# First-half projections in token order, the local recurrence stage ahead of the second half's projections, the triangular solve spread over later work, and a new order of products in two attentions

## The chip, the cores and the metric

The kernel runs on one core of one Trainium2 chip. The metric is device time in microseconds (us), from launch to end. Engines are named as the profile names them: PE (TensorE, matrix products) with PEld (its weight loads), DVE (VectorE), ACT (ScalarE), POOL (GpSimd), SP (SyncE, which here only issues DMAs). An instruction on one engine's list runs in the order in which it stands there; DMAs issued on one engine's queue are issued in order too, and an issue that must wait for its data holds back all that stand behind it.

## The reference

Two blocks, float32, 512 tokens of width 1024. The first has two layers (a neighbourhood attention A, a grouped attention B, each with a gated update behind it, "ple" in the kernel). The second is one hybrid layer: a sparse attention ("nsa") and an RWKV-7 recurrence, both fed by one projection of the same normalized activations. The change touches mainly the recurrence:

```python
prev = jnp.pad(p, ((0, 0), (1, 0), (0, 0)))[:, :-1]
p = p + shift_mu * (prev - p)                       # token shift
r, k, v, wd, ad = _split(p, (512, 512, 512, 64, 64))
w = (w0 + jnp.tanh(wd) @ w_up)                      # low-rank decay
decay = jnp.exp(-jnp.exp(-jax.nn.softplus(-w) - 0.5))
a = jax.nn.sigmoid(a0 + ad @ a_up)                  # low-rank rate
kk = heads(k * k_k); kk = kk / max(norm(kk), 1e-12)
k = k * (1.0 + (a - 1.0) * k_a)
# per token: sa = S @ -kk;  S = S*decay + sa (x) (kk*a) + v (x) k;  y = S @ r
```

## The kernel before, in words

Precision is kept by splitting each operand into a high part (`float32r`) and the rest, the low part, so that a product of activations and weights is three matmuls (high by high, high by low, low by high). A weight unit of 512 KB is loaded on SP's queue into `wraw`, ACT rounds it to `whi` (L147), and the engine in `self.lo` subtracts to get `wlo` (L148): DVE or POOL.

The program is written with tiles. A planner orders each engine's list once, before the run, from simulated costs: work emitted earlier has the higher priority, but work emitted later may be put ahead where an engine would otherwise be free in the plan. The order is then fixed.

The tokens of the first block stand in an order of their own (token 64*r + c at place 8*c + r). The recurrence needs them in natural order. `natural` (L322) rewrites the activations into it: 16 copies, eight on DVE and eight on ACT. The sequence of the stages that matter:

1. The end of the last ple (`middle_norm` gives the activations `act`, t being a block of 128 tokens).
2. `rwkv_proj_first` (L804): r, k and v of the first four heads (half 0, `hh` = 0) from the tokens in their own order, 2 x 48 matmuls of 256 columns for each of the three (`group_rows`, two token blocks at a time, `tp`). Each result is copied by ACT (L796), multiplied by `mu` on DVE (L797) and subtracted on POOL (L798), to stay in two tiles until eight DMAs (L812) write it to `d_raw`, with the order of tokens put right by the address pattern.
3. `rwkv_lowrank` (L747): 24 matmuls of 512 columns, the token shift, then eight low-rank products (L769), each with a tanh on ACT and a store to `d_low` on ACT's queue, through two buffers.
4. r of the second four heads (half 1), then in the next scope `rwkv_consts` (L724; it also writes zeros to `d_t` with eight DMAs on SP's queue, L736), k and v of half 1, `natural`.
5. `rwkv_local` (L827), eight times (`hh` = 0, 1; t = 0 to 3): it loads `low` from `d_low` (L837) and two shifted views of r, k, v from `d_raw` (L841), adds them (L844), normalizes, forms cumulative decays, and masks small products into `d_a` and others. It is a long chain that goes back and forth between DVE, ACT, POOL and PE. POOL makes the low parts of the weights here.
6. `rwkv_triangles` loads `d_a` (L951) and `rwkv_solve` (L957) inverts 128 triangles of 32 by 32 on DVE in 31 steps of two or four instructions (L967, L969), all emitted in one go; the result goes to `d_t` on ACT's queue.
7. `products()`: nsa's blocks, compression (L1186), keys, the gates of the recurrence, nsa's queries and scores. Between its pieces `tail` places the steps of the recurrence's `chain` (from `d_t`) by a list of numbers, the first behind piece 10.
8. `nsa_group` for two groups, then the output projection.

Attention B (`b_block`, L648) and nsa (`nsa_block`, L1337) transpose probabilities in pairs, split them (ACT the high part `ph`, then DVE the low part `pl`, L222), and multiply: block 0 high, block 0 low, block 1 high, block 1 low (L677, L1373).

## Time and profile before

| what | us |
|---|---|
| median of three runs | 1224.47 (1223.39 to 1226.15) |
| the profiled execution | 1225.36 |
| its span, first to last instruction | 1223.6 |
| busy in the span: PE, DVE, ACT, POOL | 1138.2, 851.1, 623.0, 395.8 |
| mean granted TensorE clock | 0.969 of full speed |

A busy PE is not PE at its peak: matmuls overlap, and the end of each is modelled, so that a PE waiting between two matmuls can still count as busy. How many matmuls start in a stretch tells more. A clock of 1.00 is 2.4 GHz, 0.5 is 1.2 GHz.

### The profile page before, as it was taken

To read this page: it belongs to the slowest core of one execution; us is meant where nothing else is said; L and a number is where in the kernel's file an instruction comes from. 1 tells how busy PE (TensorE), PEld (TensorE's weight loads), DVE (VectorE), ACT (ScalarE), POOL (GpSimd) and SP (SyncE) were. 2 spreads that over 40 slices of the span, in tenths; PEclk is the share of its full clock that TensorE was granted. 3 is DMA by queue.
4 is the path that set the end of the run, shared out by engine and by line. 5 is a ranking of instruction groups with operands and counts; after the bars stand their busy time and mean duration, and the time that the engine had idled before them with its cause. 6 is when DMAs were issued, how large, how long until landed. Compare 5 with 4: busy or idle time off the path is not lost.

```text
span 1223.6 us, 20514 instructions
## 1 busy us (share of the span) xinstructions
PE 1138.2 (93%) x7176; PEld 999.8 (82%) x7176; DVE 851.1 (70%) x2093; ACT 623.0 (51%) x1355; POOL 395.8 (32%) x549
## 2 busy tenths in 40 slices
PE   7999999998999989999999999799899799899896
PEld 5898989886889868877877898688789688798785
DVE  6566666657677877886676763489786925688865
ACT  5566565635443566566564642434444223267743
POOL 0021211110300364674311011164445523357731
PEclk9999999999999989999999999899799989899998
DMA  6333333213232310211132445774667553712511
GB/s 248 117 98 102 102 103 102 92 61 132 93 108 74 97 38 1 70 35 36 52 130 69 139 120 192 219 262 145 202 189 195 162 140 106 237 45 71 180 52 69
DMA packets 87040, 143.24 MB, mean 117 GB/s; under 512 B 21525, under 2 KB 52245, under 8 KB 86938
## 3 DMA queue, kind: packets, MB, share of 16 engines
q1 hardware_dynamic: 72344, 133.49, 34.3%
q10 hardware_dynamic: 14018, 6.36, 2.0%
q0 software_dynamic: 576, 2.10, 0.5%
q8 instruction: 56, 0.92, 0.3%
q14 instruction: 46, 0.38, 0.1%
HBM read 114.12 MB, written 27.79 MB: 116 GB/s over the span
## 4 chain that ended last, share of the span: by engine, by line
PE 61%; DVE 17%; DMA 7%; ACT 5%; issue 5%; POOL 3%; SPq 2%; ACTq 0%; POOLq 0%; DVEq 0%
PE mm L205 23%; PE mm L188 5%; PE mm L189 5%; PE mm L190 4%; PE sc L205 3%; PE mm L216 2%; DVE KT L967 2%; PE tr L492 1%; PE u L677 1%; PE tr L670 1%; DMA rkv<-d_raw 1%; PE ch L1003 1%; DVE big L969 1%; PE u L1373 1%; PE tr L318 1%
## 5 line engine op out<-in xcount | busy, mean ns | idle before, releaser
L205 PE MATMUL mm<-whi,act 128*128 128x256 f32 (+2 forms) x1344 | 356.2, 323 | 9.7 <-DVE x L347 3.5
L205 PE MATMUL mm<-wlo,act 128*128 128x256 f32 (+2 forms) x896 | 287.1, 321 | 0.5 <-POOL wlo L148 0.5
L205 PEld LDWEIGHTS mm<-whi,act 128*128 128x128 f32 x1344 | 239.8, 194 | 31.3 <-DVE x L347 5.5
L205 PEld LDWEIGHTS mm<-wlo,act 128*128 128x128 f32 x896 | 174.7, 195 | 10.3 <-POOL wlo L148 0.7
L147 ACT CAST whi<-wraw 128x1024 fp32r<-128x1024 f32 (+1 forms) x128 | 133.3, 1043 | 91.9 <-PE mm L205 38.5
L148 DVE TENSOR_TENSOR wlo<-wraw,whi 128x1024 fp32r<-128x1024 f32 x91 | 116.6, 1284 | 54.2 <-ACT whi L147 52.4
L205 PE MATMUL mm<-whi,half 128*128 128x256 f32 (+1 forms) x448 | 146.0, 327 | 4.2 <-DVE half L222 4.2
L148 POOL TENSOR_TENSOR wlo<-wraw,whi 128x1024 fp32r<-128x1024 f32 (+2 forms) x37 | 88.0, 2382 | 129.7 <-DVE rs_y L237 69.9
L188 PE MATMUL mm<-act,whi 128*128 128x512 f32 x312 | 126.1, 404 | 2.2 <-DVE b_qn L547 2.2
L190 PE MATMUL mm<-act,wlo 128*128 128x512 f32 x312 | 124.6, 399 | 0.0
L205 PEld LDWEIGHTS mm<-whi,half 128*128 128x128 f32 x448 | 88.4, 198 | 10.8 <-DVE half L222 5.1
L484 POOL TENSOR_SCALAR a_P<-a_P,a_rd 128x256 f32<-128x256 f32 x64 | 32.9, 517 | 156.5 <-DVE a_rd L483 143.9
L189 PE MATMUL mm<-half,whi 128*128 128x512 f32 x200 | 79.1, 396 | 0.0
L188 PEld LDWEIGHTS mm<-act,whi 128*128 128x128 f32 x312 | 59.9, 192 | 14.4 <-issue 3.4
L190 PEld LDWEIGHTS mm<-act,wlo 128*128 128x128 f32 x312 | 59.9, 192 | 12.2
L663 POOL TENSOR_SCALAR b_P<-b_P,b_rd 128x512 f32<-128x512 f32 x64 | 45.5, 715 | 54.6 <-DVE b_rd L662 44.0
L660 ACT ACTIVATE b_P<-sc,b_mn 128x512 f32<-128x512 f32 x64 | 44.1, 690 | 21.5 <-DVE b_mn L657 13.6
L657 DVE TENSOR_REDUCE b_mn<-sc 128x1 f32<-128x512 f32 x64 | 43.5, 684 | 10.6 <-PE sc L655 10.2
L478 DVE CUSTOM_DVE_ANT_0 a_P<-sc,a_bias 128x256 f32<-128x256 f32 x64 | 26.1, 421 | 34.7 <-PE tr L492 20.1
L1359 POOL TENSOR_SCALAR n_P<-n_P,b_rd,n_gl 128x128 f32<-128x128 f32 (+3 forms) x64 | 39.2, 619 | 30.6 <-DVE b_rd L1357 10.3
L222 DVE TENSOR_TENSOR b_pl<-tr,b_ph 128x512 fp32r<-128x512 f32 x64 | 43.3, 683 | 6.0 <-ACT b_ph L221 5.3
L189 PE MATMUL mm<-act,whi 128*128 128x512 f32 x112 | 45.8, 409 | 0.0
(396 smaller groups left out, 2826.8 us busy)
## 6 DMA issues: line engine op xcount, KB each, us to landing
wraw<-in_wstream SPq DMA_DIRECT2D x133, 512.0 KB, 3.6
a_bias<-in_bias SPq DMA_DIRECT2D x16, 384.0 KB, 3.1
rkv<-d_raw SPq DMA_DIRECT2D x16, 384.0 KB, 4.9
d_raw<-act SPq DMA_DIRECT2D x8, 384.0 KB, 5.6
xf<-x SPq DMA_DIRECT2D x4, 512.0 KB, 3.7
d_low<-low ACTq DMA_DIRECT2D x8, 256.0 KB, 2.8
d_t<-rkv SPq DMA_DIRECT2D x8, 256.0 KB, 4.2
low<-d_low SPq DMA_DIRECT2D x8, 256.0 KB, 3.3
```

Of the source, the lines that this page charges most:

```text
L147: nc.scalar.copy(hi[:, :m], raw[:, :m])
L148: self.lo.tensor_tensor(lo[:, :m], raw[:, :m], hi[:, :m].bitcast(F32), op=OP.subtract)
L188: nc.tensor.matmul(ps, lhsT=wh[:, kt], rhs=ah[:, kt], start=kt == 0, stop=False)
L189: nc.tensor.matmul(ps, lhsT=wh[:, kt], rhs=al[:, kt], start=False, stop=False)
L190: nc.tensor.matmul(ps, lhsT=wl[:, kt], rhs=ah[:, kt], start=False, stop=kt == KT - 1)
L205: nc.tensor.matmul(ps, lhsT=l, rhs=r, start=i == 0, stop=i == len(ops) - 1)
L222: (eng_lo or nc.vector.tensor_sub)(lo, src, hi.bitcast(F32))
L484: nc.gpsimd.tensor_scalar(w, w, rd, 0.5, op0=OP.mult, op1=OP.mult)
L657: nc.vector.tensor_reduce(mn, ps, axis=AX.X, op=OP.max, negate=True)
L660: nc.scalar.activation(pt, ps, AF.Exp, bias=mn, scale=1.0, accum_out=den)
L663: nc.gpsimd.tensor_scalar(pt, pt, rd, 0.5, op0=OP.mult, op1=OP.mult)
L1359: nc.gpsimd.tensor_scalar(w, w, rd, st["gl"][:, b, gc:gc + 1], op0=OP.mult, op1=OP.mult)
```

## The change

- `rwkv_proj` takes several names and goes over token pairs first, then names; ACT's copy is gone, the product with `mu` and the subtraction are both on DVE, and each half's result is stored by four DMAs of 128 KB at once. `rwkv_proj_first` is gone: only r of half 0 is still made from the tokens in their own order (`swapped`), through four small rings of tiles.
- `rwkv_lowrank` is a generator. Its loads and memsets (now on POOL) stand at its head, the token shift is one ACT and one DVE instruction instead of three on DVE, the products use all 128 rows, `d_low` is stored on SP's queue through three buffers. It is advanced up to its first yield, then `natural` is made, then the eight products, then k and v of half 0 from the tokens in natural order.
- `natural` copies by k instead of by token block; still eight copies of 512 elements on each of DVE and ACT.
- r, k, v of half 1 are all emitted behind the locals t = 0, 1, 2 of half 0; `self.lo` is POOL only from half 1's locals on. The loads of parameters stand ahead of the constants.
- The zeros for `d_t` are written in the first layer's ple (`zero_inverses`, a memset on POOL and eight DMAs on SP's queue).
- `rwkv_triangles` loads `d_a` in three parts (96, 16, 16 rows). `rwkv_solve` is a generator: four steps behind each of the first nine pieces of `products()`. Its stores go to SP's queue.
- The gates' low parts are made on DVE.
- `b_block` and `nsa_block` multiply both high blocks before both low ones.

```diff
@@ -323,12 +323,9 @@
+        for k in range(KT):
+            for a, o, copy in zip(act, out, (nc.vector.tensor_copy, nc.scalar.copy)):
+                copy(o[:, k].rearrange("p (r c) -> p r c", r=8), a[:, k].rearrange("p (c r) -> p r c", r=8))
...
@@ -671,9 +668,9 @@
-            for k in range(2):
-                kc = 2 * kp + k
-                for x, src in enumerate((ph, pl)):
+            for x, src in enumerate((ph, pl)):
+                for k in range(2):
+                    kc = 2 * kp + k
                     nc.tensor.matmul(U, lhsT=V[:, kc], rhs=src[:, k], start=kc == 0 and x == 0, stop=kc == 3 and x == 1,
                                      skip_group_check=True)
...
+    def zero_inverses(self, pool):
+        nc = self.nc
+        zero = pool.tile([P, 512], F32, name="zero", bufs=1)
+        nc.gpsimd.memset(zero, 0.0)
         for t in range(TT):
             for h in range(2):
-                nc.sync.dma_start(out=self.head_rows(self.d_t, t, 4 * h, 4), in_=zero[:, :512].rearrange("p (h n) -> p h n", h=4))
+                nc.sync.dma_start(out=self.head_rows(self.d_t, t, 4 * h, 4), in_=zero.rearrange("p (h n) -> p h n", h=4))
...
@@ -747,31 +747,40 @@
     def rwkv_lowrank(self, buf, act):
...
+        rest = self.small.tile([P, 1], F32, name="wa_rest", bufs=1)
+        nc.vector.tensor_scalar(rest, mu, -1.0, 1.0, op0=OP.mult, op1=OP.add)
+            m, one = buf[:, 3 + 2 * j], 64 - 64 * j
+            nc.gpsimd.memset(m[64 - 64 * j:128 - 64 * j], 0.0)
+            nc.sync.dma_start(out=m[64 * j:64 * j + 64], in_=self.a[up])
+            nc.sync.dma_start(out=m[one:one + 1], in_=bass.AP(tensor=self.a[row].tensor, offset=self.a[row].offset, ap=[[S, 1], [1, S]]))
+            l = buf[:, 2 + 2 * j]
+            nc.gpsimd.memset(l[64 - 64 * j:128 - 64 * j], 0.0)
+            nc.gpsimd.memset(l[one:one + 1], 1.0)
+        ps = self.cols(("r_wa",), act)
+        raw, d = buf[:, 1], buf[:, 0]
+        nc.scalar.copy(raw.rearrange("p (r t c) -> p t c r", r=8, t=TT), ps.rearrange("p (t c r) -> p t c r", t=TT, r=8))
+        nc.scalar.mul(d, raw, rest)
+        nc.vector.scalar_tensor_tensor(d[:, 1:], raw[:, :S - 1], mu, d[:, 1:], op0=OP.mult, op1=OP.add)
+
+        for j in range(2):
+            w = slice(64 * j, 64 * j + 64)
+            nc.scalar.activation(buf[w, 2 + 2 * j], d[w], AF.Tanh if j == 0 else AF.Copy)
+        for t in range(TT):
+            yield
+            for j in range(2):
-                nc.tensor.matmul(ps, lhsT=l[0:65, t * P:t * P + P], rhs=m[0:65], start=True, stop=True)
-                th = buf[:, 6 + t % 2]
+                nc.tensor.matmul(ps, lhsT=l[:, t * P:t * P + P], rhs=m, start=True, stop=True)
+                th = buf[:, (6, 7, 1)[(2 * t + j) % 3]]
...
-                nc.scalar.dma_start(out=self.d_low[j, t], in_=th)
+                nc.sync.dma_start(out=self.d_low[j, t], in_=th)
...
@@ -780,40 +789,35 @@
-                ps = self.group_rows(us, act, tp)
+    def rwkv_proj(self, act, hh, names, mu, stage, swapped=False):
+
+        nc = self.nc
+        keys = {name: [("r_" + name, hh, j) for j in range(2)] for name in names}
+        self.fetch(*sum(keys.values(), []))
+        us = {name: [self.w.pop(k) for k in keys[name]] for name in names}
+        for tp in range(2):
+            for name in names:
+                n = "rkv".index(name)
+                ps = self.group_rows(us[name], act, tp)
                 r = stage(n, tp)
                 p2 = ps.rearrange("p (t n) -> p t n", t=2)
-                m = mu[:, names.index(name), None, :].to_broadcast([P, 2, 256])
-                nc.scalar.copy(r[0], p2)
+                m = mu[:, n, None, :].to_broadcast([P, 2, 256])
                 nc.vector.tensor_tensor(r[1], p2, m, op=OP.mult)
-                nc.gpsimd.tensor_tensor(r[0], r[0], r[1], op=OP.subtract)
-                for t in range(2 * hh):
+                nc.vector.tensor_tensor(r[0], p2, r[1], op=OP.subtract)
+                for t in range(2):
                     for d, a in zip(self.d_raw[hh], r):
-                        o = bass.AP(tensor=d.tensor, offset=d.offset + (1 + 16 * (2 * tp + t)) * 768 + 256 * n, ap=[[768, 16], [64 * 768, 8], [1, 256]])
+                        o = 1 + (16 if swapped else P) * (2 * tp + t)
+                        o = bass.AP(tensor=d.tensor, offset=d.offset + 768 * o + 256 * n,
+                                    ap=([[768, 16], [64 * 768, 8]] if swapped else [[768, P]]) + [[1, 256]])
                         nc.sync.dma_start(out=o, in_=a[:, t])
...
-        par = {n: self.bcast(pool, n, 256 * hh, 256) for n in ("k_k", "k_a", "r_k")}
+        par = {}
+        for n in ("r_k", "am", "k_k", "k_a"):
+            if n != "am":
+                par[n] = self.bcast(pool, n, 256 * hh, 256)
+            elif hh == 0:
+                pool.tile([P, 256], F32, name="am", bufs=2)
...
-        nc.scalar.dma_start(out=A, in_=self.blocks(self.d_a))
+        for i, n in ((0, 96), (96, 16), (112, 16)):
+            nc.scalar.dma_start(out=A[i:i + n], in_=self.blocks(self.d_a, i, n))
...
+            yield
-            nc.scalar.dma_start(out=self.blocks(self.d_t, 32 * t, 32), in_=T[w])
+            nc.sync.dma_start(out=self.blocks(self.d_t, 32 * t, 32), in_=T[w])
...
+                        if (hf, t) == (1, 0):
+                            N.zero_inverses(pool)
...
-                    rest = N.rwkv_proj_first(act, N.rwkv_mu(pool, 0, 0, 3, "mu0"))
-                    N.rwkv_lowrank(pool.tile([P, 8, S], F32, name="low", bufs=1), act)
-                    N.rwkv_proj(act, 1, "r", N.rwkv_mu(pool, 1, 0, 1, "mu1"), lambda n, tp: [a[:, tp] for a in rest])
+                    mu = N.rwkv_mu(pool, 0, 0, 3, "mu0")
+                    names = iter(TT * (("pp", 4), ("pp", 4), ("th", 2), ("pu", 2)))
+
+                    def ring(n, tp):
+                        two = [next(names) for _ in range(2)]
+                        return [pool.tile([P, 512], F32, name=k, bufs=b).rearrange("p (t n) -> p t n", t=2) for k, b in two]
+
+                    N.rwkv_proj(act, 0, "r", mu, ring, swapped=True)
+                    low = N.rwkv_lowrank(pool.tile([P, 8, S], F32, name="low", bufs=1), act)
+                    next(low)
+                    act = N.natural(act)
+                    for _ in low:
+                        pass
+                    N.rwkv_proj(act, 0, "kv", mu, ring)
...
-                N.rwkv_consts(loc)
-                N.rwkv_proj(act, 1, "kv", N.rwkv_mu(loc, 1, 1, 3, "mu"), stage)
-                act = N.natural(act)
+                mu = N.rwkv_mu(loc, 1, 0, 3, "mu")
+                par = N.rwkv_params(loc, 0)
+                N.rwkv_consts(loc)
                 st = N.rwkv_state(N.consts)
-                N.lo = nc.gpsimd
                 for hh in range(2):
-                    par = N.rwkv_params(loc, hh)
+                    if hh:
+                        par = N.rwkv_params(loc, hh)
+                        N.lo = nc.gpsimd
                     for t in range(TT):
                         N.rwkv_local(loc, hh, t, par, st)
+                        if hh == 0 and t < 3:
+                            N.rwkv_proj(act, 1, "rkv"[t], mu, stage)
...
-            N.rwkv_solve(chn, *sv)
+            solve = N.rwkv_solve(chn, *sv)
...
+                N.lo = nc.vector
                 for _ in N.rwkv_gates(pool, act):
                     yield
+                N.lo = nc.gpsimd
...
             for n, _ in enumerate(products()):
+                for _ in range(4 if n < 9 else 0):
+                    next(solve, None)
```

## Rows read from the trace of the kernel before

**Rows 1.** Busy time by stretch: stretch, us, then busy (x instructions) of each engine.

```profile
706.00:749.00 43.00, 42.43 (x314) 40.59 (x315) 22.58 (x50) 15.64 (x23) 8.66 (x6) 0.96 0.48 145
749.00:799.00 50.00, 41.63 (x266) 36.88 (x266) 19.54 (x31) 22.07 (x28) 9.73 (x11) 0.86 0.69 211
799.00:934.40 135.40, 123.79 (x943) 113.01 (x943) 114.85 (x286) 60.98 (x196) 65.42 (x75) 0.92 0.60 191
934.40:990.00 55.60, 44.98 (x303) 40.98 (x301) 42.22 (x123) 15.12 (x21) 27.42 (x25) 0.91 0.71 182
990.00:1065.00 75.00, 70.27 (x538) 65.10 (x538) 34.64 (x77) 20.75 (x35) 21.33 (x38) 0.93 0.51 160
```

**Rows 2.** Chain of waits from 690 to 1075: start us, us, what.

```profile
720.84 22.66 PE mm L205 x189
754.61 1.72 PE sc L769 x4
...
867.34 3.18 PE mm L1186 x14
...
934.42 7.59 DMA big<-d_a
...
1020.32 0.23 PE mm L189
```

**Rows 3.** The first sum of each local: ns min/median/max, first and last start; waits.

```profile
L844 DVE TENSOR_TENSOR rkv<-rkv x8: 939/958/2044, 799.2 to 905.2; 128x768 f32<-128x768 f32 x8
...
  DMA rkv<-d_raw: 10.6, 4
```

**Rows 4.** The copies of `natural`: ns min/median/max, first and last start.

```profile
L330 ACT CAST act<-half x8: 1138/1166/1260, 770.5 to 777.9; 128x512 fp32r<-128x512 f32 x8
L330 DVE CAST act<-act x8: 622/636/686, 772.7 to 776.6; 128x512 fp32r<-128x512 f32 x8
```

**Rows 5.** Timeline of DVE: start us, us, instruction.

```profile
720.82 1.37 DVE L222 TENSOR_TENSOR half<-tr,act 128x512 fp32r<-128x512 f32 x2 [2.76 <-ACT act L221]
...
805.14 2.32 DVE L236 TENSOR_SCALAR l_i<-l_ss 128x4 int32<-128x4 int32 x1
...
826.04 0.17 DVE L236 TENSOR_SCALAR l_i<-l_ss 128x4 int32<-128x4 int32 x1
```

**Rows 6.** Timeline of POOL, beside the middle row of rows 5.

```profile
805.04 4.75 POOL L148 TENSOR_TENSOR wlo<-wraw,whi 128x1024 fp32r<-128x1024 f32 x2
```

**Rows 7.** Timeline of SP's queue ahead of the first local.

```profile
780.91 6.09 SPq L736 DMA_DIRECT2D d_t<-rkv  x8
...
789.80 2.50 SPq L802 DMA_DIRECT2D d_raw<-st  x4
792.34 1.08 SPq L841 DMA_DIRECT2D rkv<-d_raw  x2
```

**Rows 8.** DVE's groups from 799 to 934.4: busy us, mean ns.

```profile
L236 DVE TENSOR_SCALAR l_i<-l_ss 128x4 int32<-128x4 int32 x8 | 5.5, 687 | 0.2
...
L1171 DVE TENSOR_TENSOR half<-mm,n_posk 64x496 f32<-64x496 f32 x4 | 2.7, 670 | 0.0
...
L797 DVE TENSOR_TENSOR st<-mm,mu 128x512 f32<-128x512 f32 x2 | 1.4, 684 | 0.0
```

**Rows 9.** L205's matmuls alone in the same stretch.

```profile
799.00:934.40 135.40, 43.80 (x284) 37.69 (x284) 0.92 0.60 191
```

**Rows 10.** DMA issues from 700 to 990: KB each, median us to landing.

```profile
rkv<-d_raw SPq DMA_DIRECT2D x16, 384.0 KB, 4.9
...
d_raw<-st SPq DMA_DIRECT2D x16, 128.0 KB, 3.7
...
d_aq<-abq SPq DMA_DIRECT2D x16, 64.0 KB, 3.4
```

**Rows 11.** PE's waits in the two attentions: us in total, times, longest.

```profile
PE u L677 <- DVE b_pl L222: 4.8, 9, 1.3
...
PE u L1373 <- DVE n_pl L222: 4.0, 3, 2.7
```

**Rows 12.** The page's group for low parts made on DVE.

```profile
L148 DVE TENSOR_TENSOR wlo<-wraw,whi 128x1024 fp32r<-128x1024 f32 x91 | 116.6, 1284 | 54.2 <-ACT whi L147 52.4
```

43 lines of the change are left out of this document (4 added, 39 removed).

## The prediction, made before the changed kernel ran

> **What bounds the kernel now.** I read the table by stretch first, for where PE starts few matmuls. From 706 to 749 it starts 314 in 43 us; from 799 to 934.4, the stretch of the eight locals, 943 in 135 us; there DVE is busy 114.9 of 135.4 us, and the clock is granted at 0.92 of full [rows 1]. The chain of waits gives the pace of a PE that never waits: 189 matmuls of 256 columns in 22.66 us, 0.12 us each, and 0.23 us each for 512 columns [rows 2]. At that pace the 284 projection matmuls of the local stretch would take 34 us [rows 9], so PE has room there, while the local chain goes through DVE and its own loads. The first sum of a local starts at 799.2, the last at 905.2, about 15 us apart, and DVE waits 10.6 us for the views of `d_raw` that it sums [rows 3]. So from 706 to 1065 the end is set by three things in turn: when the first local can start, how long the eight last, and what products PE still owes afterwards. The profiled execution took 1225.36 us for a span of 1223.6 us, 1.8 us outside it, 0.9 us over the median of 1224.47; the sum is made on it. Two executions that differ by under 0.2% (2.4 us) I count as the same.
>
> **The start of the first local** (799.2 before). Before it PE now does r of half 0 (96 matmuls, 11.5 us), the low-rank column (24 x 0.23 = 5.5), eight low-rank products (16 records at 1.72/4, 6.9) and k, v of half 0 (192, 23.0) [rows 2]. Moved behind it: 288 matmuls of half 1. The reordered tokens are now on the way to k and v: the last normalized block is split at 720.82 + 1.37 = 722.2 [rows 5], ACT's eight copies at 1.17 us end at 731.5, DVE's at 0.64 earlier [rows 4]. Until then PE has r and the column, 17 us, which covers the wait. The first pair of token blocks of k and v then takes 11.5 us plus about half of the low-rank products, 3.5: 746.5. Behind it come two DVE instructions of 0.68 [rows 8], four store issues, 2.5 us, two load issues, 1.1 [rows 7], the store's 3.7 and the load's 4.9 us to landing [rows 10]. Sum: 746.5 + 1.4 + 2.5 + 3.7 + 1.1 + 4.9 = 760.1. The zeros' eight issues, 6.09 us of SP right ahead of the first loads [rows 7], are gone from here, and so is the wait of the loads behind them. This is 39 us earlier; I take 38, since ACT and SP serve more than this. Bounds: 25 if the k, v stage runs wholly behind the low-rank products and the second pair (6.9/2 + 11.5 later), 44 if the copies hide behind the end of ple.
>
> The memsets of the low-rank stage go from DVE to POOL, which has 9.7 us of work in 50 [rows 1]; products over 128 rows instead of 65 have the same columns and I take the same time; the nearest other bound is nothing. Stores of `d_low` add eight issues to SP, about 5 us, but end the ACT list's wait for two buffers; both lie beside PE's work.
>
> **The eight locals** (135.2 us before, 799.2 to 934.4). Into them go r, k, v of half 1: six halves with two DVE instructions of 0.68, 8.2 us, of which two, 1.4, were there [rows 8]; and six low parts, which DVE makes in 1.28, 7.7 [rows 12]. Together +14.5 on DVE. Out of them go POOL's subtraction and ACT's copy. What POOL's low parts cost DVE is seen in one place: while POOL makes two of them (805.04, 4.75 us) [rows 6], the small integer step L236 takes 2.32 us where it takes 0.17 elsewhere [rows 5]. Its mean is 0.687 over eight [rows 8]; with its twin L237 at the same cost, 16 x 0.52 = 8.3 us is what could come back; I take 4, since POOL's other work stays. The Trainium skill, page "SBUF — State Buffer", section "SBUF: two separate sides", says that GpSimd and VectorE share a pair of ports as an exclusive lock, which whoever starts first holds for its whole instruction, the other one blocked; a VectorE instruction with two SBUF inputs takes it too. By that rule, with which the 2.32 beside the 4.75 agrees, low parts moved to VectorE lock out GpSimd instead, and that is a rival below. The products' own DVE work in this stretch, eight sums of 0.67 (L1171) [rows 8] and others, about 10 us by my estimate, is partly pushed out by work of higher priority: half, 5. So +14.5 - 4 - 5 = +5.5: 140.7 us. From below, all three reliefs in full and the 20.5 us that DVE idles [rows 1] mostly used: 118. From above, no relief and DVE held up as now: 157.
>
> **What is left behind the locals** (130.6 us before, 934.4 to 1065). PE did products during the locals: 284 less 96 of the last projection, 188 x 0.12 = 22.6; 48 columns x 0.23 = 11.0; 128 compression matmuls, which the chain shows at 3.18/14 = 0.23 in a stretch at half the clock, so about 0.11, 14.5 [rows 2, 9]. That is 48. Half 1's 34.6 us now stand in their place, 11.5 of which were there already, so 23 us of products pass behind the locals. But there they find room: from 934.4 to 990 DVE, with the solve, is busy 42.2 of 55.6 us, and PE starts only 303 matmuls [rows 1], which at full pace are some 41 us. The displaced ones (keys, compression) ask little of DVE, and the solve now stands between them by four steps instead of ahead of them: of the 15 us of room I give back 11 (bounds 0 and 15). The load of `d_a`, 7.59 us between the last local and the solve [rows 2], is cut: its last part is 64 KB, for which the nearest row is 3.4 us [rows 10]; 3 us saved (0 to 4.2). The gates' four low parts go from about 2.4 on POOL to 1.28 on DVE where DVE waits for ACT anyway: nothing, or up to 5 us on DVE if the solve is still running. So +23 - 11 - 3 = +9.
>
> **The rest.** In the two attentions PE waits nine times for `pl` of B (4.8 us) and three times for that of nsa (4.0) [rows 11]. In each such wait one matmul more of 0.12 us can be done: 1.4; over all 104 pairs it would be 12.5. I take 2, nearer to the row. The zeros move to the first layer, where 6.1 us of issues [rows 7] stand ahead of weight loads on SP: between 0 and 6; I take 1, because three buffers of weights lie ahead of PE there.
>
> Sum: -38 + 5.5 + 9 - 2 + 1 = -24.5. On the profiled execution, 1225.36 - 24.5 = 1200.9; against the median, 1200.0. I say 1200.
>
> **Rivals.**
>
> *The gain is larger.* What speaks for it is that DVE and PE both idle in the local stretch and behind it, and that half 1's projections need nothing from the locals. Locals in 122 us, the solve's 15 us of room filled, 3 saved: -38 - 13 + 23 - 15 - 3 - 1 = -47, 1178. Against it: the loads' waits of 10.6 us [rows 3] stay.
>
> *VectorE becomes the bound and the gain is eaten.* DVE is at 85% in the local stretch [rows 1] and gets 14.5 us more. If its six low parts also hold POOL up (7.7 us), on whose products the local chain waits, and nothing is relieved: +22 there, +23 behind it with 5 of the room used and 3 saved, -38 and -1: -2, 1222. The Trainium skill's rule above is the one that speaks for this. Against it: POOL's own low parts of 2.4 us each are gone from half 0.
>
> *Slower: SP's queue holds the locals' loads back.* Half 1's 24 stores are issued on the same queue as each local's three loads. If the order puts each half's four stores, which wait for its 48 matmuls (5.8 us) and DVE's 1.4, ahead of the next local's loads, six waits of 7.2 us come into the chain: +43, 1243. It decides from 4.1 us a half on (24.5/6). For it: the loads of `d_raw` are already what DVE waits for. Against it: the projection's priority is below that of the local ahead of it, and two views can be loaded ahead.
>
> *The order hardly changes,* because the planner pulled later work forward before too: then only start and end shift and the sum is that of the second rival; I count it there.
>
> **How the numbers follow.** Forecast 0.52 (its own range 1186 to 1214), larger gain 0.22 (1160 to 1186), gain eaten 0.10 (1214 to 1229, half of it within 0.2% of before), slower 0.16 (1227 to 1260). Faster: 0.52 + 0.22 + 0.04 = 0.78. Within 0.2%: 0.05. Slower: 0.17. The range reaches from 1168, with some 0.06 below, into the slower case up to 1231, with some 0.13 above.
>
> **What would show it.** The first sum L844 (a line or so on) should start near 761, with r's, k's, v's matmuls of half 1 between the locals' small products, not ahead of them; the eight locals should last near 141 us; the solve's steps should be spread, with PE starting over 6 matmuls a microsecond beside them. DVE's L236 twin pair in half 0 should fall to about 0.17. It would be wrong if the first local starts after 775 (copies or stores late), if SP shows stores of half 1 waiting ahead of loads, if POOL's products wait for DVE's low parts, or if the chain from `d_t` starts so late that PE stands still for it.

## The result and the profile after

| | before | after |
|---|---|---|
| median, us | 1225.31 (4 runs) | 1203.36 (4 runs, 1199.19 to 1210.13) |
| profiled execution: us, span | 1225.36, 1223.6 | 1202.5, 1200.6 |
| busy: PE, DVE, ACT, POOL | 1138.2, 851.1, 623.0, 395.8 | 1132.4, 840.5, 617.1, 376.8 |

The ratio is 0.983 [0.980, 0.985]: some 21 us faster, against 24.5 forecast; the two profiled spans differ by 23.0. Where it came from is read by markers, the same instructions in both traces:

| marker, us from the span's start | before | after | shift |
|---|---|---|---|
| attention B's first product with V | 440.9 | 440.9 | 0.0 |
| last scaled block of x, the end of ple | 719.3 | 714.2 | -5.1 |
| first local's sum starts | 799.2 | 766.3 | -32.9 |
| last local's last mask ends | 930.2 | 911.8 | -18.4 |
| solve, first step | 942.1 | 925.9 | -16.2 |
| solve's result first applied | 990.2 | 970.3 | -19.9 |
| `n_Vp` of the NSA attention starts | 1064.8 | 1044.6 | -20.2 |
| last `og` ends | 1151.5 | 1128.4 | -23.0 |

(`n_Vp` is the copy of the compressed values with which the NSA attention begins, `og` the recurrence's output times its gate; the solve's result is applied in the first product with what was stored to `d_t`.) Between any two rows the difference of the shifts is what that stretch gained or lost. Two windows of after between such markers (columns as in [rows 1]):

```profile
766.30:911.80 145.50, 137.76 (x1036) 127.75 (x1034) 116.40 (x294) 58.79 (x183) 57.86 (x61) 0.89 0.59 183
911.80:1044.60 132.80, 120.14 (x897) 112.11 (x897) 75.86 (x206) 40.72 (x69) 48.50 (x71) 0.95 0.63 181
```

and two of before between the same markers:

```profile
799.20:930.20 131.00, 119.39 (x907) 108.61 (x905) 114.10 (x285) 59.44 (x189) 65.42 (x75) 0.92 0.61 193
930.20:1064.80 134.60, 119.25 (x875) 110.08 (x873) 77.35 (x200) 37.40 (x63) 48.55 (x62) 0.92 0.59 167
```

In the stretch of the locals PE starts 1036 matmuls in 145.5 us where it started 907 in 131.0; behind it 897 in 132.8 against 875 in 134.6. So the 23 us of products which the prediction moved behind the locals are hardly there: 22 more matmuls, not some 190. PE did all of half 1's work beside the locals (its last stores to `d_raw` are issued from 808.3 on), and these lasted longer. DVE got little more, 116.4 us against 114.1 of busy time.

The sums of the locals (duration min/median/max; first and last start; waits):

```profile
L848 DVE TENSOR_TENSOR rkv<-rkv x8: 943/958/1932, 766.3 to 877.2; 128x768 f32<-128x768 f32 x8
...
  DMA rkv<-d_raw: 4.8, 3
  DMA d_kb<-rt: 3.4, 1
```

and DVE's two small integer steps in the locals (busy us, mean ns):

```profile
L236 DVE TENSOR_SCALAR l_i<-l_ss 128x4 int32<-128x4 int32 x8 | 2.5, 307 | 0.2
L237 DVE TENSOR_SCALAR l_y<-l_i 128x4 int32<-128x4 int32 x8 | 1.6, 198 | 0.0
```

Against [rows 3] DVE waits 4.8 us for `d_raw` instead of 10.6 (before one of the sums it stands 3.4 us more, which the trace puts down to another DMA), and against [rows 8] the twin steps cost 307 and 198 ns instead of 687: 16 steps, 7 us back on DVE, as the prediction's rule from [rows 5, 6] had it.

What held the first local shows in the timeline of SP's queue, first the first pair of token blocks of v, then the second and what follows:

```profile
738.87 0.79 SPq L812 DMA_DIRECT2D d_raw<-pu  x2
739.75 0.89 SPq L812 DMA_DIRECT2D d_raw<-th  x2
...
753.78 0.79 SPq L812 DMA_DIRECT2D d_raw<-pu  x2
754.66 0.90 SPq L812 DMA_DIRECT2D d_raw<-th  x2
755.62 0.44 SPq L789 DMA_DIRECT2D mu<-in_shift_mu  x1
...
758.09 0.43 SPq L725 DMA_DIRECT2D rkv<-in_ind  x1
...
759.04 0.94 SPq L845 DMA_DIRECT2D rkv<-d_raw  x2
```

The first pair's v is stored from 738.87 to 740.64, some 10 us earlier than the prediction had it; the copies of `natural` on ACT, for which it waited, end at 719.3 instead of 731.5. But the queue goes in order: the stores of the second pair, which wait for PE and DVE until 754.5, stand ahead of six loads of parameters, 755.62 to 758.52, and these ahead of the first local's own, 18 us behind the last store that it needs.

Why the last local took 34.6 us (877.2 to 911.8; before 25.0) shows in the chain of waits, of which these are pieces (start us, us, what):

```profile
893.33 1.63 PE x L924 x24
...
895.94 1.28 PE mm L1192 x12
...
898.57 2.14 PE mm L205 x16
...
903.51 1.73 PE mm L1192 x16
905.24 1.63 PE x L924 x24
```

L924 belongs to the local. Between its parts the chain runs through L205 and L1192, the window's keys and the compression: PE works in the order of its list, and the last local's small products stand behind them. In the 145.5 us PE's own waits come to 7.5 us in all, in the 131.0 us before to 11.4; the windows above say the same (PE busy 137.76 of 145.50 us and 119.39 of 131.00).

### The profile page after: what moved, and what is told of

Same layout as the page of the kernel before. It is cut to its first block, busy times and chain, and to the rows that moved or that the text cites. A ratio compares the mean times of both kernels' runs of the same rounds, so it can differ in the third digit from the quotient of the medians.

```text
span 1200.6 us, 20540 instructions
## 1 busy us (share of the span) xinstructions
PE 1132.4 (94%) x7176; PEld 997.1 (83%) x7176; DVE 840.5 (70%) x2105; ACT 617.1 (51%) x1344; POOL 376.8 (31%) x540
## 5 line engine op out<-in xcount | busy, mean ns | idle before, releaser
L205 PE MATMUL mm<-whi,act 128*128 128x256 f32 (+2 forms) x1504 | 371.8, 320 | 5.9 <-DVE x L344 2.5
L205 PE MATMUL mm<-wlo,act 128*128 128x256 f32 (+2 forms) x896 | 289.0, 323 | 7.0 <-POOL wlo L148 6.3
L205 PEld LDWEIGHTS mm<-whi,act 128*128 128x128 f32 x1504 | 260.0, 194 | 28.1 <-DVE x L344 4.0
L205 PEld LDWEIGHTS mm<-wlo,act 128*128 128x128 f32 x896 | 174.3, 195 | 19.3 <-POOL wlo L148 6.5
L147 ACT CAST whi<-wraw 128x1024 fp32r<-128x1024 f32 (+1 forms) x128 | 133.3, 1043 | 87.3 <-DMA wraw<-in_wstream 25.5
L188 PE MATMUL mm<-act,whi 128*128 128x512 f32 x312 | 124.5, 399 | 2.3 <-DVE b_qn L544 2.3
L148 POOL TENSOR_TENSOR wlo<-wraw,whi 128x1024 fp32r<-128x1024 f32 (+2 forms) x33 | 78.7, 2388 | 101.3 <-DVE rs_y L237 69.9
L205 PE MATMUL mm<-whi,half 128*128 128x256 f32 (+1 forms) x288 | 98.5, 342 | 4.0 <-DVE half L222 4.0
L205 PEld LDWEIGHTS mm<-whi,half 128*128 128x128 f32 x288 | 55.8, 194 | 10.1 <-DVE half L222 5.4
L654 DVE TENSOR_REDUCE b_mn<-sc 128x1 f32<-128x512 f32 x64 | 43.4, 683 | 11.0 <-PE sc L652 10.5
L475 DVE CUSTOM_DVE_ANT_0 a_P<-sc,a_bias 128x256 f32<-128x256 f32 x64 | 26.1, 421 | 34.7 <-PE tr L489 20.2
L221 ACT CAST b_ph<-tr 128x512 fp32r<-128x512 f32 x64 | 36.8, 585 | 22.5 <-PE tr L667 22.1
L1365 POOL TENSOR_SCALAR n_P<-n_P,b_rd,n_gl 128x128 f32<-128x128 f32 (+3 forms) x64 | 39.4, 621 | 28.2 <-DVE b_rd L1363 19.8
```

The lines of the kernel that those rows point to most:

```text
L147: nc.scalar.copy(hi[:, :m], raw[:, :m])
L148: self.lo.tensor_tensor(lo[:, :m], raw[:, :m], hi[:, :m].bitcast(F32), op=OP.subtract)
L188: nc.tensor.matmul(ps, lhsT=wh[:, kt], rhs=ah[:, kt], start=kt == 0, stop=False)
L205: nc.tensor.matmul(ps, lhsT=l, rhs=r, start=i == 0, stop=i == len(ops) - 1)
L654: nc.vector.tensor_reduce(mn, ps, axis=AX.X, op=OP.max, negate=True)
L1365: nc.gpsimd.tensor_scalar(w, w, rd, st["gl"][:, b, gc:gc + 1], op0=OP.mult, op1=OP.mult)
```

## The experiments

Each kernel was timed beside the kernel before on its own chip; the intervals below are of the ratio to it. Differences from after are worked out as the difference of the ratios from 0.983 times 1225, and are good to some 4 to 6 us (both intervals together). The markers are of the profiled execution of each; the solve is taken from the start of its first step to that of its last:

| kernel | ratio | against after, us | first sum | last mask | solve, us | result applied | `n_Vp` | `og` ends |
|---|---|---|---|---|---|---|---|---|
| after | 0.983 [0.980, 0.985] | | 766.3 | 911.8 | 31.4 | 970.3 | 1044.6 | 1128.4 |
| r_order_only | 0.997 [0.995, 0.999] | (3.3 under before) | 794.5 | 930.4 | 39.0 | 991.3 | 1067.8 | 1152.0 |
| r_order_undone | 0.988 [0.985, 0.991] | +6.4 | 772.7 | 915.5 | 31.7 | 974.0 | 1048.9 | 1132.9 |
| p_proj_first | 0.990 [0.987, 0.992] | +8.2 | 768.9 | 915.6 | 39.0 | 976.1 | 1041.4 | 1132.3 |
| l_low_pool | 0.994 [0.992, 0.997] | +14.1 | 770.8 | 911.4 | 41.1 | 975.0 | 1060.5 | 1144.5 |
| s_solve_at_once | 0.983 [0.979, 0.987] | +0.5 | 766.0 | 909.6 | 32.2 | 968.0 | 1043.7 | 1129.0 |
| z_zeros_late | 0.990 [0.987, 0.993] | +9.1 | 773.0 | 917.1 | 42.1 | 981.2 | 1055.0 | 1139.0 |
| d_load_whole | 0.986 [0.982, 0.989] | +3.3 | 765.9 | 910.1 | 33.9 | 968.6 | 1043.5 | 1128.4 |
| q_queries_dve | 0.983 [0.980, 0.986] | +0.2 | 767.4 | 910.9 | 40.8 | 978.7 | 1038.0 | 1139.0 |
| c_consts_act | 0.989 [0.986, 0.991] | +7.5 | 768.6 | 913.4 | 41.9 | 978.4 | 1055.0 | 1138.4 |
| k_sp_clear | 0.989 [0.986, 0.991] | +7.0 | 769.1 | 908.6 | 37.4 | 970.8 | 1048.9 | 1132.6 |
| a_stores_act | 0.989 [0.986, 0.992] | +7.0 | 767.6 | 918.1 | 38.8 | 978.5 | 1050.7 | 1140.6 |
| g_gates_pool | 0.987 [0.985, 0.990] | +5.6 | 765.4 | 908.3 | 34.2 | 963.0 | 1048.4 | 1135.9 |

The planner makes the lists anew for each kernel, and the traces show how far an edit reaches. In s_solve_at_once every engine has the same instructions in the same order as in after (7176 matmuls, 2105 instructions of DVE, 1344 of ACT, 540 of GpSimd, and the DMA issues): it is after once more, and its row shows how well markers repeat, to some 2.5 us. d_load_whole differs from after in a few places only. In every other kernel made from after, the lists differ from near the edit on, also where the edit does not reach. In c_consts_act, for one, GpSimd makes a low part at 929.42, ahead of its memset at 932.46; in after the memset comes first, at 930.32, and the low part at 936.86. So these differences are of the edit and of the new order together.

**The attentions' order, alone and undone.**

```diff
-            for k in range(2):
-                kc = 2 * kp + k
-                for x, src in enumerate((ph, pl)):
+            for x, src in enumerate((ph, pl)):
+                for k in range(2):
+                    kc = 2 * kp + k
```

(and the same in the NSA attention; in r_order_only put into the kernel before, in r_order_undone taken out of after)

> The kernel before, with the new order of high and low products in the two attentions and nothing else of the change. Theory: attention B ended 6.6 us earlier (628.26 to 621.65) and the NSA attention ran 2.9 us shorter after the change, and both come from this reorder alone: 8 to 9.5 us faster, about 1216, with the first local's sum near 792. Rival, the prediction's own term: only the waits that the trace names are filled by one matmul more each, 1.4 to 2 us: about 1223; attention B's 6.6 us then came from other work being planned differently around it. Third possibility: the rest of the kernel waits for something else from 706 on and gives the gain back: attention B ends near 622, but the total moves by under 3 us.

> The kernel after, with the old order of products in both attentions. Theory: 8 to 9.5 us slower than after, about 1212, still some 13 us faster than before: this is then the share of all the rest of the change (against a predicted 22.5). Rival (the reorder is worth the predicted 2): about 1205, and the rest of the change is worth about 20.

Attention B's high and low products with V: r_order_only, then r_order_undone (duration min/median/max, first and last start).

```profile
L677 PE MATMUL u<-b_ph,b_V x128: 274/282/386, 442.7 to 623.1; 128*128 128x256 f32 x128
...
L677 PE MATMUL u<-b_pl,b_V x128: 274/283/387, 442.9 to 624.5; 128*128 128x256 f32 x128
```

```profile
L674 PE MATMUL u<-b_ph,b_V x128: 274/282/415, 442.5 to 630.2; 128*128 128x256 f32 x128
...
L674 PE MATMUL u<-b_pl,b_V x128: 274/283/389, 442.6 to 630.3; 128*128 128x256 f32 x128
```

From first to last they take 181.8 us with the new order and 187.8 with the old; before (440.9 to 628.1) and after (440.9 to 622.8) agree. So the reorder is worth 5.3 to 6.0 us in B, in both kernels: 0.08 to 0.09 us in each of 64 pairs of blocks, not one matmul in each of the nine waits that [rows 11] name. Of those 4.8 us after has

```profile
PE u L674 <- DVE b_pl L222: 1.9, 5, 0.6
```

so that 2.9 us of the gain can be named. In the NSA attention the runs disagree: from `n_Vp` to the last `og` it is 84.2 us in r_order_only, 2.5 less than before, but 84.0 undone and 83.8 after. Alone the reorder brought 3.3 us of the 8 to 9.5 expected, undone it cost 6.4. Where the rest went in r_order_only, as far as its profiled execution shows (1225.34 us, over its median of 1222.52): the locals last 135.9 us instead of 131.0 with nearly the same instructions, at a granted clock of 0.86 instead of 0.92, and what is behind them 137.4 instead of 134.6.

```profile
794.50:930.40 135.90, 127.09 (x916) 116.84 (x916) 114.69 (x285) 60.77 (x189) 66.10 (x76) 0.86 0.62 189
```

What made the clock fall there was not tried.

**Half 1's projections ahead of the locals.**

```diff
+                for n in "rkv":
+                    N.rwkv_proj(act, 1, n, mu, stage)
                 for hh in range(2):
...
-                        if hh == 0 and t < 3:
-                            N.rwkv_proj(act, 1, "rkv"[t], mu, stage)
```

> The kernel after, with r, k, v of half 1 written ahead of the loop of locals instead of behind the first three (the first half's early r, k, v and the early loads stay). Theory: PE then does half 1's 288 matmuls, 34.6 us by the prediction's pace, with a higher priority than the locals' small products, DVE their 8.2 us; the locals start at the same 766 but the first ones are stretched, and the products which then follow the locals are fewer: the total is 5 to 20 us slower than after. Rival: the order written hardly matters, since the queue of PE is full up to the locals' start anyway and the same work is done by the locals' end: within 3 us of after.

8 us slower, which is in the expected range, but not in the locals: 146.7 us with 1040 matmuls, as after. `n_Vp` even starts 3 us earlier; what came later is the solve's end and the application of its result (+5.8). The order written for these projections is thus not what sets the length of the locals; the cost fell behind them, where the solve lasts 39.0 us.

**Low parts on GpSimd: half 1's, then the gates'.**

```diff
+                N.lo = nc.gpsimd          # l_low_pool: ahead of the locals' loop
                 for hh in range(2):
```

```diff
-                N.lo = nc.vector          # g_gates_pool: around the gates
                 for _ in N.rwkv_gates(pool, act):
                     yield
-                N.lo = nc.gpsimd
```

> The kernel after, with the low parts of half 1's r, k, v projections (six of 1.28 us on VectorE) made by GpSimd, as before the change. Theory A, the locals last 145.5 us against the predicted 140.7 because DVE got this work: the locals get up to 7.7 us shorter, the total 2 to 6 us faster. Theory B, GpSimd at work holds small VectorE steps up (2.32 us beside a GpSimd low part of 4.75 us, 0.17 without): the locals get longer, the total 2 to 8 us slower. Theory C, DVE, busy 79% of the local stretch, is no bound there, and the loads (d_low 23.7 us of waits of ACT, d_raw 4.8 of DVE) are: within 2 us of after.

> The kernel after, with the gates' four low parts back on GpSimd. Theory, from the runs so far: while GpSimd makes a low part, VectorE's two-input steps stand still (in the solve of the kernel after, four steps take 4.78 + 1.30 us instead of 0.46 a pair beside GpSimd's 4.75 us; the solve's own steps sum to 26 us with no low part on GpSimd beside them, to 31 in the kernel after, to 39 where GpSimd is busy 21 us). One of the four gates' low parts lies in the solve and three just ahead of it; on GpSimd, at 2.4 us each and later, two to three of them fall into the solve: its steps last 35 to 39 us, the application of its result starts 5 to 8 us later, and the total is 5 to 8 us slower, near 1210. Rival, the prediction's own term: nothing, since DVE waits for ACT there and the solve has room: within 2 us of after. Other side: VectorE, free of four times 1.22 us, finishes the solve earlier: 2 to 4 us faster.

l_low_pool: the locals did get 5 us shorter (140.6), with 75 fewer matmuls beside them. The 14 us that the total lost, more than any of the theories had, are behind them, 149.1 us for 132.8, in which PE starts 978 matmuls for 897:

```profile
911.40:1060.50 149.10, 133.63 (x978) 125.87 (x977) 79.34 (x211) 43.85 (x75) 48.32 (x68) 0.92 0.58 168
```

So here the products were displaced, and the last of the keys' among them: ACT's copies of these products, which the keys' rotation on GpSimd (L1123) needs, have their last start at 912.0 in after and at 927.8 here (after, then l_low_pool), and the rotation and the products that need it come 17 us later.

```profile
L1147 ACT COPY st<-mm x7: 258/265/272, 840.9 to 912.0; 128x128 f32<-128x128 f32 x7
```

```profile
L1147 ACT COPY st<-mm x8: 260/266/271, 850.4 to 927.8; 128x128 f32<-128x128 f32 x8
```

```profile
928.28 1.33 POOL L994 MEMSET big<- 32x256 f32 x4 [25.53 <-DVE wlo L148]
929.70 0.43 POOL L1123 TENSOR_TENSOR rope<-st,rope 128x64 f32<-128x64 f32 x1
```

The memset that GpSimd has ahead of the rotation stands for 25.5 us (it writes into the tile into which `d_a` is loaded, an issue of 923.62), but it holds the rotation up only from 928.1, when the copy is done, to 929.7. g_gates_pool was 5.6 us slower, as expected in size but not in way: the solve began and ended earlier, its result was applied 7.3 us earlier (963.0), and yet `n_Vp` came 3.8 us later. PE's longest waits there, and then those of after:

```profile
PE mm L1156 <- POOL st L1128: 5.7, 1, 5.7
PE ch L1009 <- DMA big<-d_t: 3.4, 1, 3.4
PE mm L205 <- DVE st L404: 2.8, 1, 2.8
```

```profile
PE mm L205 <- POOL wlo L148: 6.3, 1, 6.3
PE mm L1156 <- POOL st L1128: 2.4, 1, 2.4
```

The keys' products wait 5.7 us for GpSimd's rotation instead of 2.4: ACT had its input ready at 909.44, and GpSimd made two of the gates' low parts until 911.83. The two waits below it are new, the 6.3 us for a low part are gone; all in all PE waits 17.4 us here for 13.2, at a granted clock of 0.91 for 0.95. So the prediction's zero for the gates was too small, by some 5 us with the error given above, and "GpSimd holds VectorE up in the solve" (34.2 us for 31.4) was not what decided.

**The solve and its surroundings.**

```diff
-            solve = N.rwkv_solve(chn, *sv)        # s_solve_at_once
+            for _ in N.rwkv_solve(chn, *sv):
+                pass
...
-        for i, n in ((0, 96), (96, 16), (112, 16)):   # d_load_whole
-            nc.scalar.dma_start(out=A[i:i + n], in_=self.blocks(self.d_a, i, n))
+        nc.scalar.dma_start(out=A, in_=self.blocks(self.d_a))
...
-                N.lo = nc.gpsimd                  # q_queries_dve, behind the gates
```

> The kernel after, with the solve written in one go ahead of the products, as before the change, instead of four steps ahead of each of nine products. The prediction's term: 11 us of the room behind the locals is filled because the solve stands between the products; without it the total is 8 to 13 us slower, about 1213, the products' sums and low parts on DVE come after the solve, and the solve itself gets shorter (it took 31.3 us, 26 of them its own instructions). Rival: the order by priority puts DVE's product work between the solve's steps either way, or PE has enough products in hand that need nothing from DVE: within 3 us of after. Other side: the solve ends earlier, the chain from its result starts earlier, up to 5 us faster.

> The kernel after, with d_a loaded in one piece instead of three. The prediction's term: 3 us slower (0 to 4.2), the gap from the last mask to the solve's first step, 14.1 us after the change, grows to 17. Rival, from the trace of after: that gap was 11.9 before the change with one load and did not shrink with three, because three issues of ACT's queue and the last piece's 4.39 us take what the smaller load saves: within 1.5 us of after, with a gap of 12 to 14.

> The kernel after, with the low parts of the NSA queries' weights, which follow the gates, on VectorE as well instead of GpSimd. After the change PE stands still for 6.6 us (942 to 949) for one such low part, which GpSimd makes behind a sum that waits for the load of d_v. Theory: this gap goes and the total is 3 to 6 us faster, about 1199. Rival: DVE is busy 24.9 of 31 us there with the solve; each low part of 1.22 us that it makes holds the solve up, and the chain from the solve's result, not PE, sets the end from 957 on: between no change and 4 us slower.

Writing the solve at once left the lists as they were, as the first rival had it, so this run cannot tell what spreading the solve is worth. But in neither kernel is it spread. Here are the windows of the solve, before and then after:

```profile
942.00:980.70 38.70, 29.53 (x213) 27.37 (x212) 37.83 (x115) 8.50 (x12) 21.89 (x23) 0.92 0.61 181
```

```profile
925.90:957.30 31.40, 24.72 (x183) 24.18 (x182) 30.04 (x111) 6.24 (x8) 12.32 (x11) 0.89 0.68 207
```

Of DVE's 115 and 111 instructions all but seven and four are steps of the solve, and PE starts 5.5 matmuls a microsecond beside it before, 5.8 after, not over 6 as predicted. With one load of `d_a` the gap between the last mask and the solve is 15.2 us instead of 14.1 (13.8 in s_solve_at_once), and the total +3.3 is within what can be told. The solve itself shows what sets its length; DVE's groups over the solve of after, of q_queries_dve and of c_consts_act (below):

```profile
L974 DVE TENSOR_TENSOR big<-big,KT 128x135 f32<-128x135 f32 (+37 forms) x53 | 16.5, 342 | 0.2
L972 DVE TENSOR_TENSOR KT<-big,big 128x135 f32<-128x135 f32 (+37 forms) x54 | 14.4, 296 | 1.2 <-DMA big<-d_a 0.9
```

```profile
L972 DVE TENSOR_TENSOR KT<-big,big 128x135 f32<-128x135 f32 (+37 forms) x54 | 13.1, 273 | 2.2 <-DMA big<-d_a 1.9
L974 DVE TENSOR_TENSOR big<-big,KT 128x135 f32<-128x135 f32 (+37 forms) x54 | 13.0, 268 | 0.3
L148 DVE TENSOR_TENSOR wlo<-wraw,whi 128x1024 fp32r<-128x1024 f32 x7 | 8.8, 1257 | 3.8 <-ACT whi L147 3.8
```

```profile
L974 DVE TENSOR_TENSOR big<-big,KT 128x135 f32<-128x135 f32 (+37 forms) x54 | 20.1, 402 | 0.3
L972 DVE TENSOR_TENSOR KT<-big,big 128x135 f32<-128x135 f32 (+37 forms) x54 | 19.3, 386 | 5.6 <-DMA big<-d_a 5.3
```

Its 108 steps are the same in all. The two groups add up to 26.1 us in q_queries_dve, 30.9 in after and 39.4 in c_consts_act, while GpSimd is busy 10.5, 12.3 and 21.7 us beside them (before: 36.7 and 21.9). A step takes 0.27 us in the median. Steps of over 0.8 us: none in q_queries_dve, where GpSimd makes no low part in the solve, four in after (7.6 us together), six before (12.7), seven in c_consts_act (15.4), each beside a low part of GpSimd or its sum L1109 (L1103 before). One such place of after, DVE's timeline, then GpSimd's:

```profile
944.93 0.46 DVE L974 TENSOR_TENSOR big<-big,KT 128x96 f32<-128x96 f32 x2
945.32 1.30 DVE L972 TENSOR_TENSOR KT<-big,big 128x88 f32<-128x88 f32 x2
946.55 4.78 DVE L974 TENSOR_TENSOR big<-big,KT 128x88 f32<-128x88 f32 x2
...
951.62 0.44 DVE L974 TENSOR_TENSOR big<-big,KT 128x80 f32<-128x80 f32 x2
```

```profile
946.42 4.75 POOL L148 TENSOR_TENSOR wlo<-wraw,whi 128x1024 fp32r<-128x1024 f32 x2
```

Pairs of steps that take 0.46 us ahead of it and 0.44 behind take 1.30 and 4.78 beside GpSimd's two low parts. The Trainium skill, page "SBUF — State Buffer", section "SBUF: two separate sides", gives the pair of ports of the two engines as an exclusive lock; these rows agree. (In l_low_pool the 41.1 us of the solve are of another kind: 13 other instructions of DVE stand between its steps, four in after, and DVE idles 5 us.) In q_queries_dve seven low parts, 8.8 us, moved out of GpSimd into DVE's own queue, and the solve ended 9.2 us later; `n_Vp` started 6.6 us earlier, and `og` ended 10.6 later (the span 4.1, the median no later). This speaks for two chains that end close together: in most kernels of the table `og` ends 83 to 88 us behind `n_Vp`; where that is longer (p_proj_first, q_queries_dve, a_stores_act) it ends 156 to 162 us behind the first application of the solve's result. After the change it is 83.8 and 158.1, so that neither chain seems to have room against the other. This is read from the markers; no run holds one chain still. The 6.3 us in which PE stands still around 945 could not be had by this edit.

**SP's queue ahead of the first local.**

```diff
-                        if (hf, t) == (1, 0):                # z_zeros_late
-                            N.zero_inverses(pool)
...
                 N.rwkv_consts(loc)
+                zero = loc.tile([P, 768], F32, name="rkv", bufs=4)
+                nc.vector.memset(zero, 0.0)
+                for t in range(TT):
+                    for h in range(2):
+                        nc.sync.dma_start(out=N.head_rows(N.d_t, t, 4 * h, 4), in_=zero[:, :512].rearrange("p (h n) -> p h n", h=4))
...
-            nc.sync.dma_start(out=raw, in_=self.a[name].rearrange("p a n -> p (a n)") if n > 2 else self.a[name])
+            nc.scalar.dma_start(out=raw, in_=self.a[name].rearrange("p a n -> p (a n)") if n > 2 else self.a[name])
...
-                        nc.sync.dma_start(out=o, in_=a[:, t])
+                        (nc.scalar if tp and not hh else nc.sync).dma_start(out=o, in_=a[:, t])   # k_sp_clear
...
-                        nc.sync.dma_start(out=o, in_=a[:, t])
+                        (nc.scalar if hh else nc.sync).dma_start(out=o, in_=a[:, t])   # a_stores_act
```

c_consts_act changes the queue of `tri` and `ind` as shown, and that of `mu`, `r_k`, `k_k` and `k_a` in the same way; k_sp_clear has this and the edit marked so.

> The kernel after, with the zeros of d_t written where they were before, behind the constants of the locals, from a tile of the locals' pool, so that SP issues their eight stores (6.09 us before) right ahead of the first local's work. The prediction's term: the first local's loads wait behind them, the first sum moves from 766 to 770 to 772 and the total is 4 to 6 us slower. Rival: the first sum waits for k and v of half 0, on which PE is full until 764.7, and the zeros' issues fall into SP's idle time ahead of the stores: within 2 us of after.

> The kernel after, with the six loads of parameters and constants ahead of the first local (mu, r_k, k_k, k_a, tri, ind) issued by ACT's queue instead of SP's. After the change SP issues them one behind the other from 755.62 to 758.56, between the last store of half 0's v and the first local's loads, while ACT idles 15.9 us. Theory: what holds the first local is SP's queue in its order, the last store and all that stands behind it; then the first sum starts 2.9 us earlier (with the eight zeros back in the same place it started 6.7 us later) and the total is 2 to 4 us faster, about 1200. Rival: the loads wait for the last stores of v to land, or for the buffers that these free, whatever the queue; the first sum moves by under 1 us and the total stays within 2 us of after.

> As the run before it, and the stores of the second pair of token blocks of half 0 (r, k, v, twelve) also go to ACT's queue. Theory (the prediction's step that the first local waits for the first pair only, spoilt by SP's order): the first pair's v is through DVE at about 751 or earlier, and the first local's loads pass the second pair's stores, so that the first sum starts 8 to 12 us earlier, near 756, and the total is 5 to 10 us faster. Rival 1: the loads wait for all twelve stores by their tracking, so only the six loads' 2.9 us come back. Rival 2: the stores keep ACT's own work waiting (weights' high parts, the first local's casts): no gain or 1 to 5 us slower.

> The kernel after, with the 24 stores of half 1's r, k, v on ACT's queue instead of SP's. The prediction's slower rival: they hold the locals' loads up on SP. After the change one such hold is seen (four stores from 760.32 to 765.37 ahead of the second and third local's loads), and the locals' starts 3 to 7 are as far apart as before the change. Theory: one hold of about 5 us, off the chain because the third local starts at 781 and the fourth waits for buffers: within 2 us of after. Rival: each half's stores cost the locals something: 4 us or more faster. Other side: ACT, whose instructions then wait for DVE's sums ahead of its own casts for the locals, is held up: 3 to 10 us slower.

With the zeros back the first sum starts 6.7 us later. SP's timeline of z_zeros_late:

```profile
759.77 0.47 SPq L845 DMA_DIRECT2D rkv<-d_raw  x1
760.34 7.48 SPq L1574 DMA_DIRECT2D d_t<-rkv  x8
767.92 1.49 SPq L845 DMA_DIRECT2D rkv<-d_raw  x1
```

The zeros' eight issues stand between the first local's two loads: what the prediction put at 6.1 us is 6.7 us in the first sum, and 9.1 in the total, in which the solve of 42.1 us has a part too. Moving the six loads away did not bring the 2.9 us back. ACT's queue and then SP's in c_consts_act:

```profile
756.65 0.34 ACTq L683 DMA_DIRECT2D k_k<-in_k_k  x1
760.22 0.33 ACTq L683 DMA_DIRECT2D k_a<-in_k_a  x1
```

```profile
757.41 0.54 SPq L1134 DMA_DIRECT2D rope<-in_rope_n  x1
761.34 0.33 SPq L812 DMA_DIRECT2D d_raw<-st  x1
761.71 1.34 SPq L845 DMA_DIRECT2D rkv<-d_raw  x2
```

In after the six loads follow the stores on SP 0.5 us apart; on ACT's queue they pause, 3.2 us before `k_a` and 1.1 before `ind`, for what the trace does not name. But the local's own loads were held by something else: ahead of them on SP there now stands a store of half 1's r, which waits until DVE has its data, at 761.34. In after that store stands behind the loads, at 760.32. So the loads of `d_raw` are issued at 761.71 instead of 759.04, and the first sum comes 2.3 us later. With the second pair's stores on ACT too (k_sp_clear) it is the same: a store of half 1, issued at 762.86 behind DVE, then the local's loads at 763.24, and the sum at 769.1. DVE's work on half 1 waits there for `mu`, which stands behind the moved stores on ACT's queue (756.55). Both kernels were some 7 us slower, more than expected. So neither run shows how early the first local could start with SP's queue clear; what they show is the prediction's slower rival, a store of half 1 ahead of a local's loads, put there by the new order.

Half 1's stores on ACT's queue made the kernel 7.0 us slower, as the "other side" had it: the locals took 150.5 us, and ACT's own work in them waits for these stores in two places (L935 4.0 us behind DVE's `st`, L874 3.6 us behind `d_raw<-st`). PE starts 1059 matmuls in them for 1036, which may have a part. SP's queue thus sets when the first local starts, but nothing was gained by taking work from it.

## Why the prediction was right, and where it was not

The direction held, and the main mechanism: a first local that starts some 30 us earlier, part of which is paid back in the locals. The size (-23.0 on the profiled spans against -24.5) came this close by luck: start and locals were 10 and 9 us worse than forecast, what is behind them and the attentions 11 and 6 us better.

| step of the sum | predicted | measured on the profiled spans |
|---|---|---|
| start of the first local, from the end of ple | -38 | -27.8 |
| eight locals | +5.5 | +14.5 |
| left behind the locals, to `n_Vp` | +9 | -1.8 |
| attentions: up to the end of ple, and from `n_Vp` on | -2 | -5.1 and -2.9 |
| zeros in the first layer | +1 | 0.0 (attention B starts at 440.9 in both) |

- *Start.* The step from the first pair to the first local's loads failed. The first pair of v was stored by 740.6, where the sum has 750.4, but from there to the loads it took 18.4 us for 3.7: between them SP's order puts the second pair's stores and six loads. In c_consts_act and k_sp_clear, which move these, a store of half 1 took their place, so that the price of the order alone is not measured. The term's lower bound, 25, was the one for a stage that runs behind the second pair, and there it came out. That the zeros cost their 6 us right there was shown by z_zeros_late.
- *Locals.* "PE has room there" failed. 129 more matmuls started in 14.5 more us, 0.11 us each, about the full price at the 0.12 of [rows 2]; the same lists took 143.6 us in s_solve_at_once at a granted clock of 0.92, which is the clock of before: 0.10 us each. The room had been read from 284 of the 943 matmuls; PE's waits between the same markers are 7.5 us after the change and 11.4 before. l_low_pool, with six low parts less on DVE and 75 matmuls less on PE, had locals 4.9 us shorter, which by itself cannot tell the two apart; behind them 81 more matmuls and 16.3 more us followed. p_proj_first, with the same matmuls earlier, had them as long. The clock has a part as well: r_order_undone did 1036 matmuls in 142.8 us at 0.96.
- *Behind.* "+23 of displaced products" failed for the same reason: they were not displaced. "-11, the solve spread" failed too: the solve is no more spread than before (seven other instructions of DVE in it, then four), and PE starts 5.8 matmuls a microsecond beside it for 5.5. What shortened this stretch is the solve, 31.4 us for 38.6, in which GpSimd's work holds up four steps instead of six; of the 3 us of the split load 1 is seen, no more than markers scatter. Taken together, locals and what is behind them came to +12.7 against +14.5.
- *Gates* at "nothing" were worth some 5 us (g_gates_pool). One wait of PE that is 3.3 us longer comes by way of GpSimd's order; from where the rest comes is not settled.
- *Reorder*: 5 to 6 us in attention B where 2 were taken, and the other bound was 12.5; the trace's named waits were too few to count by. Whether the -2.9 from `n_Vp` on comes from the reorder is open: alone it brings 2.5 there, yet with the order undone the gain stays.
- *Rivals.* The slower one (half 1's stores hold the locals' loads) was among the prediction's signs of being wrong. In after it appears once, 760 to 765; in c_consts_act and k_sp_clear it holds the first local itself; and moving half 1's stores away made the kernel slower. VectorE as the bound did not come: busy 80% of the local stretch, 87% before. The 5 to 10 us by which the work around the solve moves with edits far from it go with the planner's new orders. What stays open is what each edit would do with all other lists kept, and how far PE and how far DVE's chain sets the length of a local.

No kernel tried beats the one after the change.

## What to carry to other kernels

Before work is moved into a stretch because an engine "has room" there, add up that engine's waits between the same two markers: if they are few microseconds, new instructions cost their full time, however few start per microsecond. When an end is set by two chains that finish close together, cost each of them to its end, since shortening one alone can show nothing, as in q_queries_dve. In a queue that works in order, ask for each moved item what it will stand in front of: here two low parts ahead of the keys' rotation, a store ahead of a local's loads, and eight stores of zeros ahead of a load, in kernels that were 6, 7 and 9 us slower. And where a planner orders the lists, compare the lists of two kernels before a difference in time is put down to the edit: one edit here changed no list, others changed lists far from where they stand.

## What the runs showed of the hardware that was not expected

A VectorE instruction with two inputs beside a GpSimd low part does not slow down, it stands still: a pair of 0.46 us took 4.78 beside 4.75 us, and the steps of a solve took 26.1 us with no low part on GpSimd beside them, 39.4 with 21.7 us of GpSimd work. GpSimd is held up in turn: the sum L1109 took 3.16 us in the solve of after and 1.12 in c_consts_act, a rotation step that mostly takes 0.32 us took 1.07 at 912.33, beside one of VectorE's low parts of 1.23. Longest in z_zeros_late, beside the steps of the solve, of which DVE does one behind the other:

```profile
950.91 5.82 POOL L1123 TENSOR_TENSOR rope<-st,rope 128x64 f32<-128x64 f32 x1 [1.82 <-ACT st L1257]
```

DVE did more than twenty steps in that time, so that GpSimd was held up there by more than one instruction.
